# Where the sums of v's weights are made: from the first v product, four parts of 1024 columns, to the first u and g product, eight parts of 512

## The chip, the cores and the metric

The kernel runs on one core of a Trainium2 chip. The metric is the device time of one execution in microseconds (us), as the median of several runs. The engines are named as in the profile: PE is TensorE's matmul side, PEld its weight loads, DVE is VectorE, ACT is ScalarE, POOL is GpSimd, SP is SyncE, which here only issues DMAs. L12 is line 12 of the kernel file. Lines of the changed file are given with the words "of the changed kernel", since they are shifted by one or by six.

## The reference

Two layers act on x of 2048 tokens by 1024 features. The first is a gated MLP whose gate mixes the tokens of a chunk, the second is windowed attention. Only the first matters here:

```python
z = h @ w_in                       # 2048x1024 @ 1024x6144
u, v, g = jnp.split(z, 3, axis=-1) # 2048 wide each
v = layer_norm(v, ln_g, ln_b)
sv = jnp.einsum('gts,bcsgd->bctgd', wsm, v) + bs...   # per chunk of 128 tokens
y = u * sv * jax.nn.silu(g)
return y @ w_out
```

`h` is the RMS norm of x. Everything is float32, with an error that asks for more than one float32r pass.

## The kernel before

**Precision.** Every operand of a large product is split into a high float32r part (a CAST on ACT) and a low part (a subtraction on DVE); `split` does both, L118 and L119. A product is then three matmuls: high by high, high by low, low by high.

**Seven products for eight.** Most products are made as two by two blocks with seven block products (`chain_of`, L519), named "11", "12", "s2", "s1", "s3", "s4", "22". The blocks of both sides have first to be added and subtracted. For x, and for the gated y, this is `combos` (L365): four POOL operations (L373, L375, L379, L381) with seven DMAs that store the results (L367). For the weights of u, g and the output product it is done on POOL as they are fetched (L223 to L226, four operations for each weight tile).

**The order of the first layer.** The tokens are taken in two halves, `sb` 0 and 1.

- The first v product (`vphase_first`, L591) has no combinations: 64 steps of 12 matmuls each, one weight tile of 128x512 a step. Meanwhile x is loaded and normed, and `x_steps` (L424) makes x's combinations for the later products (DVE L451 and L452, then `combos`).
- The first u and g product follows: eight calls of `ug_pair` (L642), called a pair below, each with 14 weight tiles of 12 matmuls. In a pair, the previous pair's gate is worked out (`mix`, L628, with PE L635 and DVE L637, L639, L640) and its y combined on POOL (`combos`). In each of the fourth to seventh pair one quarter of the second half's x is combined as well (`x_steps(1, k)`, DVE L448, POOL `combos`).
- The output product, and then the same for `sb` = 1, whose v product (`vphase`, L573) is made with seven block products. Its weights' sums are read from `sumD` in DRAM. They are what the change moves.

**The sums of v's weights.** `sum_job(i)` (L465), i from 0 to 3, loads four blocks of w_v of 128x1024 into two large tiles `qa` (the places of x's "11" set, which is not loaded yet), and after two steps `quarter_sums` (L475) does four operations with two POOL instructions each (L479) and stores each result with one DMA issued by POOL (L472). That is 32 POOL operations and 16 POOL DMAs in all. They are kept in an order of their own by `in_turn`.

**What sets the order.** `after(n, fn)` calls `fn` n steps later; a step is one call of `half()`, that is 12 matmuls. Tile code emits instructions in that order, and a scheduler then fixes the row of each engine. Each engine takes its row strictly in order. Weight tiles are fetched three steps ahead (`LOOKAHEAD`), with four buffers `wa` of split weights (`W_BUFS`) and twelve of raw ones (`RAW_A`). Small tiles of 128x512 called `s` come from a pool of 18 (`GEN_A`); a load into such a tile waits on SP's row until the tile's former user is through, and what stands behind it on SP waits too.

```python
        for i in range(4):
            after(14 + 9 * i, lambda i=i: sum_job(i))          # L785, within the first v product
        ...
        for k in range(4):
            for i, f in enumerate(x_steps(1, k, None)):
                after(14 * (k + 3) + 5 + i, f)                 # L811, within the first u and g product
```

Of the kernel before, what the change touches and what calls it, by code (L numbers as in the profile page):

```python
# [12 lines left out]
F32 = mybir.dt.float32  # L13
# [3 lines left out]
ALU = mybir.AluOpType  # L17

P = 128
# [32 lines left out]
PLAIN = ("11", "12", "21", "22")  # L52
PIECES = "k00 k01 q00 q01 g00 q10 q11 g01 q20 q21 g10 q30 q31 g11 g20 g21 g30 g31".split()
ATT = [11, 12, 14, 15, 18, 20, 20, 22, 23, 26, 28, 28, 29, 31, 33, 35]
S_T = 4
T_PV = 3
K_T = 5
# [5 lines left out]
def trunk(ctx: ExitStack, tc: tile.TileContext, xT, wv, wug, wao, wkv, wqg, wbo, wsT, bs, gains, lngb,  # L63
          bq, bkv, sinks, rot, masks, out):
    nc = tc.nc
    V, A, G, PE = nc.vector, nc.scalar, nc.gpsimd, nc.tensor

    glob = ctx.enter_context(tc.tile_pool(name="glob", bufs=1))
    xcg = ctx.enter_context(tc.tile_pool(name="xcg", bufs=1))
# [10 lines left out]
    sumD = [[dram.tile([P, 2, 512], F32, name=f"su{i}_{n}", tag=f"su{i}_{n}") for n in range(4)] for i in range(4)]  # L80
# [7 lines left out]
    def load(dst, src):  # L88
        nc.sync.dma_start(dst, src)

    def slot(dt=F32):
        return gen[0].tile([P, TB], dt, name="s", tag="s")
# [49 lines left out]
    def after(n, fn):  # L142
        at(now[0] + n, fn)
# [18 lines left out]
    for b in range(NB):  # L162
        for p in PIECES:
            kind, i, j = p[0], int(p[1]), int(p[2])
# [168 lines left out]
    with ExitStack() as actx:  # L333
# [128 lines left out]

            return [begin, lambda: None, lambda: None, lambda: norms(0), lambda: norms(1), step, step, step]

        def sum_job(i):  # L465

            t = [xcg.tile([P, 2048], F32, name="qa", tag=tag) for tag in ("11h", "11l")]
            a11, a12, a21, a22 = (t[z // 2][:, (z % 2) * 1024:(z % 2 + 1) * 1024] for z in range(4))
            for t, q in ((a21, 2), (a22, 3), (a11, 0), (a12, 1)):
                load(t.rearrange("p (u c) -> p u c", u=2),  # L470
                     wv[i // 2, q, 2 * (i % 2):2 * (i % 2) + 2].rearrange("u p c -> p u c"))
            after(2, lambda: quarter_sums(a11, a12, a21, a22, lambda n, t: G.dma_start(  # L472
                sumD[i][n], t.rearrange("p (u c) -> p u c", u=2))))

        def quarter_sums(a11, a12, a21, a22, put):  # L475
            def tt(out, a, b, op):
                for z in range(2):
                    zs = slice(z * 512, (z + 1) * 512)
                    in_turn(lambda: G.tensor_tensor(out[:, zs], a[:, zs], b[:, zs], op))  # L479

            tt(a22, a21, a22, ALU.add)
            put(0, a22)
            tt(a21, a11, a21, ALU.subtract)
            put(2, a21)
            tt(a11, a22, a11, ALU.subtract)
            put(1, a11)
            tt(a12, a12, a11, ALU.subtract)
            put(3, a12)


        pre_jobs = [(wkv[i], wkvD[i], kv_g[:, 4 * i:4 * i + 4], 4) for i in range(2)]
# [265 lines left out]
        def in_turn(fn):  # L757

            if gl[0] is None:
                gl[0] = fn().ins  # L760
                return
            with tc.issue_after(gl[0]):
                gl[0] = fn().ins
# [17 lines left out]
        for k in range(KD):  # L781
            after(1 + k // 2, lambda k=k: ys.append(first_x(1, k)))
            after(3 + k // 2, lambda k=k: first_split(1, k, ys[k]))
            after(6 + k // 2, lambda k=k: first_stat(1, k, ys[k], 2))
        for i in range(4):  # L785
            after(14 + 9 * i, lambda i=i: sum_job(i))
        for k in range(4):
            for i, f in enumerate(x_steps(0, k, ("12h", "12l", "s2h", "s2l")[k])):
                after(17 + 8 * k + i, f)
# [6 lines left out]
        for sb in range(2):  # L796
# [8 lines left out]
            pend = None  # L805
            res = {}
            if sb == 0:
                for b in range(2, 4):
                    for i, f in enumerate(stat_steps(b)):
                        after(3 + 16 * (b - 2) + 3 * i // 2, f)  # L810
                for k in range(4):  # L811
                    for i, f in enumerate(x_steps(1, k, None)):
                        after(14 * (k + 3) + 5 + i, f)
# [321 lines left out]
    for b in range(NB):  # L1135
# [15 lines left out]
        def attend(i, b=b, qT=qT, os_=os_, finish_quad=finish_quad):  # L1151
# [14 lines left out]

            after(S_T, second)

        for i in range(16):
            at(h0 + ATT[i], lambda i=i, f=attend: f(i))  # L1170
        if b + 1 < NB:
# [3 lines left out]
        for p in PIECES:  # L1175
            kind, i, j = p[0], int(p[1]), int(p[2])
# [79 lines left out]
```

## Time and profile before

| what | value |
|---|---|
| median of 3 runs | 2219.04 us (2216.8 to 2220.34) |
| the profiled execution | 2223.57 us, its span 2221.8 us, 1.8 us lie around it |
| granted TensorE clock, mean | 0.983 |
| first v product | from 5.6 to 226.1 us of the span |
| first u and g product | from 226.1 to about 563 us |
| POOL operations L479 | 32, from 30.0 to 147.4 us, median 1404 ns |
| POOL DMAs L472 | 16, median 579 ns to issue, median 4.0 us to land |

In a row of the timeline stand the start and the length in us, then engine, line, operation, the tile that is written and the tile that is read, and the count of merged instructions; in brackets the idle time of the engine ahead of it and what ended it. A row of windows has the length of the stretch, for each engine its busy time with the number of instructions, the granted clock of TensorE, the busy share of the 16 DMA engines and GB/s. A row of groups ends with the busy time and the mean length in ns of one instruction, and then the idle time ahead of it.

### The profile page before, as it was taken

What the parts mean: (1) busy time and instruction counts of PE and PEld (TensorE: products, weight loads), DVE (VectorE), ACT (ScalarE), POOL (GpSimd) and SP (SyncE); (2) the same over time, 40 slices, a digit from 0 to 9 for tenths busy, and PEclk for the clock granted to TensorE, in tenths of its full rate; (3) what the DMA queues carried; (4) which work ended last, traced back from release to release, by engine and by line L of the source; (5) the groups of instructions that cost most, each with busy time, mean ns of one, the idle gap of its engine ahead of it and who ended that gap; (6) DMA issues with size and microseconds to landing.
All of it is one profiled execution on the core that took longest, in us unless ns stands there. A gap on an engine that the chain in (4) does not pass through costs nothing.

```text
span 2221.8 us, 33592 instructions
## 1 busy us (share of the span) xinstructions
PE 2133.6 (96%) x11196; PEld 1809.7 (81%) x11196; DVE 1687.7 (76%) x2693; ACT 1089.2 (49%) x2431; POOL 1065.4 (48%) x1178
## 2 busy tenths in 40 slices
PE   7799999999899999999999899999999999999997
PEld 5578888888688777788888688898899889889986
DVE  9976778888986865766657987578867967986785
ACT  5225654445444534545444543257535834663573
POOL 3781446767544566644544445334415613451460
PEclk8899999999999999999999999999999999999999
DMA  8997555667786799634435796542463354346322
GB/s 290 318 348 243 169 183 182 197 209 242 265 297 224 265 326 330 211 117 147 154 110 157 250 324 206 197 141 102 140 225 114 127 195 163 114 128 243 115 96 95
DMA packets 208940, 441.95 MB, mean 199 GB/s; under 512 B 22656, under 2 KB 61824, under 8 KB 199552
## 3 DMA queue, kind: packets, MB, share of 16 engines
q1 hardware_dynamic: 163488, 255.76, 35.6%
q0 software_dynamic: 40672, 175.66, 21.7%
q10 hardware_dynamic: 4608, 8.39, 1.0%
q8 instruction: 89, 1.46, 0.3%
q14 instruction: 83, 0.68, 0.1%
HBM read 322.81 MB, written 116.92 MB: 198 GB/s over the span
## 4 chain that ended last, share of the span: by engine, by line
PE 45%; DVE 8%; issue 3%; ACT 2%; DMA 2%; POOL 1%; SPq 0%; DVEq 0%; POOLq 0%; ACTq 0%
PE ps L122 7%; PE ps L124 6%; PE ps L123 6%; PE ps L130 6%; PE ps L129 6%; PE ps L128 6%; PE ps L1019 2%; PE ps L997 1%; PE ps L635 1%; PE ps L966 1%; PE ps L967 1%; PE ps L938 1%; DVE hn L119 1%; DVE o L1027 1%; DVE wa L119 1%
## 5 line engine op out<-in xcount | busy, mean ns | idle before, releaser
L119 DVE TENSOR_TENSOR wa<-w_raw,wa 128x512 fp32r<-128x512 f32 x456 | 465.2, 1029 | 156.4 <-ACT wa L118 153.2
L130 PE MATMUL ps<-xh,wa 128*128 128x512 f32 x1344 | 529.5, 394 | 17.7 <-DVE wa L119 17.7
L128 PE MATMUL ps<-xh,wa 128*128 128x512 f32 x1344 | 530.9, 395 | 1.3 <-ACT s L549 1.0
L129 PE MATMUL ps<-xl,wa 128*128 128x512 f32 x1344 | 527.9, 393 | 0.0
L118 ACT CAST wa<-w_raw 128x512 fp32r<-128x512 f32 x456 | 280.5, 618 | 405.8 <-PE ps L130 303.7
L130 PEld LDWEIGHTS ps<-xh,wa 128*128 128x128 f32 x1344 | 253.2, 188 | 78.7 <-DVE wa L119 22.4
L128 PEld LDWEIGHTS ps<-xh,wa 128*128 128x128 f32 x1344 | 253.5, 189 | 57.1 <-ACT s L549 1.4
L129 PEld LDWEIGHTS ps<-xl,wa 128*128 128x128 f32 x1344 | 253.4, 189 | 55.6
L1005 POOL TENSOR_SCALAR_AFFINE_SELECT s<-s 128x512 fp32r<-128x512 f32 x256 | 185.3, 752 | 101.8 <-ACT s L999 69.5
L122 PE MATMUL ps<-w,hn 128*128 128x256 f32 x640 | 184.2, 288 | 0.0
L223 POOL TENSOR_TENSOR w_raw<-w_raw 128x512 f32<-128x512 f32 x48 | 75.0, 1565 | 226.0 <-DMA w_raw<-in_wug 134.3
L123 PE MATMUL ps<-w,hn 128*128 128x256 f32 x640 | 182.3, 285 | 0.0
L124 PE MATMUL ps<-w,hn 128*128 128x256 f32 x640 | 182.2, 285 | 0.0
L119 DVE TENSOR_TENSOR xl<-s,xh 128x512 fp32r<-128x512 f32 x168 | 137.4, 853 | 15.0 <-ACT xh L118 14.5
L190 POOL DMA_DIRECT2D w<-wb x72 | 40.6, 565 | 208.3 <-PE ps L124 182.6
L631 ACT ACTIVATE vp<-vp,nb,rs 128x128 f32<-128x128 f32 x256 | 106.7, 485 | 56.6 <-DMA vp<-v 47.8
L991 POOL TENSOR_TENSOR s<-s,rd 128x512 f32<-128x512 f32 x64 | 69.6, 1090 | 115.1 <-ACT s L999 47.0
L123 PEld LDWEIGHTS ps<-w,hn 128*128 128x128 f32 x640 | 124.0, 194 | 0.5
L122 PEld LDWEIGHTS ps<-w,hn 128*128 128x128 f32 x640 | 124.0, 194 | 0.5
L124 PEld LDWEIGHTS ps<-w,hn 128*128 128x128 f32 x640 | 123.9, 194 | 0.0
L123 PE MATMUL ps<-wa,xh 128*128 128x512 f32 x256 | 104.7, 409 | 19.0 <-DVE wa L119 18.9
L225 POOL TENSOR_TENSOR w_raw<-w_raw 128x512 f32<-128x512 f32 x48 | 66.3, 1386 | 103.2 <-DVE wa L119 102.2
(190 smaller groups left out, 5011.4 us busy)
## 6 DMA issues: line engine op xcount, KB each, us to landing
w<-wb POOLq DMA_DIRECT2D x72, 1024.0 KB, 5.3
w_raw<-in_wug SPq DMA_DIRECT2D x160, 256.0 KB, 3.3
w_raw<-in_wv SPq DMA_DIRECT2D x88, 256.0 KB, 5.4
s<-in_xT SPq DMA_DIRECT2D x80, 256.0 KB, 4.8
w_raw<-in_wao SPq DMA_DIRECT2D x80, 256.0 KB, 4.1
wb<-s POOLq DMA_DIRECT2D x72, 256.0 KB, 5.8
vp<-v SPq DMA_DIRECT2D x32, 512.0 KB, 4.6
Y_s<-s POOLq DMA_DIRECT2D x64, 256.0 KB, 3.9
```

The source lines that it names most:

```text
L118: A.copy(hi, src)
L119: (lo_eng or V).tensor_tensor(lo, src, hi.bitcast(F32), ALU.subtract)
L122: PE.matmul(ps, ah, bh, start=first, stop=False)
L123: PE.matmul(ps, ah, bl, start=False, stop=False)
L124: PE.matmul(ps, al, bh, start=False, stop=last)
L128: PE.matmul(ps, ah, bh, start=first, stop=False, skip_group_check=True)
L129: PE.matmul(ps, ah, bl, start=False, stop=False, skip_group_check=True)
L130: PE.matmul(ps, al, bh, start=False, stop=True, skip_group_check=True)
L223: G.tensor_tensor(u["22"], u["21"], u["22"], ALU.add)
L631: A.activation(v[:, c, :], v[:, c, :], AF.Identity, bias=nb[:, c:c + 1], scale=rs[:, c:c + 1])
L991: G.tensor_tensor(p4, p4, rd[:, :, None].broadcast_to([P, 4, P]), ALU.mult)
L1005: G.affine_select(out=y.rearrange("p (h q) -> p h q", h=4), in_=x.rearrange("p (h q) -> p h q", h=4), pattern=[[0, 4], [sign, P]], base=ba ...
```

## The change

The four jobs of 1024 columns become eight of 512, `sum_job(i, u)`. They use four tiles `s` each in place of the two large ones. Their steps are listed in `SUMS`, counted from the start of the first u and g product: 37 and 41 lie at the end of the third pair, 55 and 58 around the border of the fourth and fifth, 69 and 72 of the fifth and sixth, 83 and 86 of the sixth and seventh. The sums follow three steps after the loads. The 32 POOL operations stay 32, each of the same size; the POOL DMAs become 32, of 256 KB in place of 512 KB; the loads become 32 of 256 KB in place of 16 of 512 KB. `in_turn` is no longer used for them.

```diff
+SUMS = (37, 41, 55, 58, 69, 72, 83, 86)
...
-        def sum_job(i):
-            t = [xcg.tile([P, 2048], F32, name="qa", tag=tag) for tag in ("11h", "11l")]
-            a11, a12, a21, a22 = (t[z // 2][:, (z % 2) * 1024:(z % 2 + 1) * 1024] for z in range(4))
+        def sum_job(i, u):
+            a11, a12, a21, a22 = (slot() for _ in range(4))
             for t, q in ((a21, 2), (a22, 3), (a11, 0), (a12, 1)):
-                load(t.rearrange("p (u c) -> p u c", u=2),
-                     wv[i // 2, q, 2 * (i % 2):2 * (i % 2) + 2].rearrange("u p c -> p u c"))
-            after(2, lambda: quarter_sums(a11, a12, a21, a22, lambda n, t: G.dma_start(
-                sumD[i][n], t.rearrange("p (u c) -> p u c", u=2))))
...
+                load(t, wv[i // 2, q, 2 * (i % 2) + u])
+            def tt(n, out, a, b, op):
+                G.tensor_tensor(out, a, b, op)
+                G.dma_start(sumD[i][n][:, u, :], out)
+            def sums():
+                tt(0, a22, a21, a22, ALU.add)
+                tt(2, a21, a11, a21, ALU.subtract)
+                tt(1, a11, a22, a11, ALU.subtract)
+                tt(3, a12, a12, a11, ALU.subtract)
+            after(3, sums)
...
-        for i in range(4):
-            after(14 + 9 * i, lambda i=i: sum_job(i))
...
             if sb == 0:
+                for i in range(8):
+                    after(SUMS[i], lambda i=i: sum_job(i // 2, i % 2))
```

POOL's row early in the first v product, before. `r_474` and `r_650` are the inverse norms of the two token blocks, `su` a stored sum, `X` a stored combination of x:

```order
L119 TENSOR_TENSOR s<-s 128x512
L260 TENSOR_TENSOR r_474<-m_471,neghalf 128x4
L479 TENSOR_TENSOR qa<-qa 128x512 x2
L472 DMA su_0_153<-qa 128x1024
L479 TENSOR_TENSOR qa<-qa 128x512 x3
L472 DMA su_2_155<-qa 128x1024
L479 TENSOR_TENSOR qa<-qa 128x512 x2
L472 DMA su_1_154<-qa 128x1024
L479 TENSOR_TENSOR qa<-qa 128x512
L472 DMA su_3_156<-qa 128x1024
L119 TENSOR_TENSOR s<-s 128x512
L367 DMA X_11_169<-xq 128x512
```

Here a whole job of eight operations and four stores stands between the two norms, and more of them follow behind each other down to the end of the row's part for the v product. The same place in the changed kernel:

```order
L120 TENSOR_TENSOR s<-s 128x512
L261 TENSOR_TENSOR r_474<-m_471,neghalf 128x4
L120 TENSOR_TENSOR s<-s 128x512
L368 DMA X_11_169<-xq 128x512
L261 TENSOR_TENSOR r_650<-m_647,neghalf 128x4
L368 DMA X_12_170<-xq 128x512
```

Nothing is left between the two norms but the split of the second one's sum.

POOL's row where the fifth pair begins, before. `X_22` is the last store of x's combinations of the pair before, `w_raw` the weights of u and g (L225 makes what "s2" multiplies, L226 what "s4" does, L223 and L224 belong to the next pair):

```order
L380 TENSOR_TENSOR s<-s 128x512
L367 DMA X_s_180<-s 128x512
L381 TENSOR_TENSOR s<-s 128x512
L367 DMA X_22_182<-s 128x512
L225 TENSOR_TENSOR w_raw<-w_raw 128x512 x2
L226 TENSOR_TENSOR w_raw<-w_raw 128x512 x2
L223 TENSOR_TENSOR w_raw<-w_raw 128x512
L224 TENSOR_TENSOR w_raw<-w_raw 128x512
L367 DMA Y_0_11_183<-s 128x512
```

The four operations on the weights follow each other here. The same place in the changed kernel, where L473 and L474 are the sums and their stores, and L226 and L227 the former L225 and L226; the first of the two jobs that stand here is shown:

```order
L368 DMA X_22_182<-s 128x512
L226 TENSOR_TENSOR w_raw<-w_raw 128x512
L473 TENSOR_TENSOR s<-s 128x512
L226 TENSOR_TENSOR w_raw<-w_raw 128x512
L474 DMA su_0_157<-s 128x512
L473 TENSOR_TENSOR s<-s 128x512
L474 DMA su_2_159<-s 128x512
L473 TENSOR_TENSOR s<-s 128x512
L227 TENSOR_TENSOR w_raw<-w_raw 128x512
L474 DMA su_1_158<-s 128x512
L473 TENSOR_TENSOR s<-s 128x512
L474 DMA su_3_160<-s 128x512
```

Eight sums and eight stores now stand between the first L225 of a pair and the L223 of the next; the same is found at the starts of the sixth and seventh pair, and at the start of the fourth the two jobs begin just ahead of the first L225.

SP's row at the same place in the changed kernel; before, the rows are the same without the one that reads `in_wv`, and all five `w_raw` follow each other:

```order
L90 DMA w_raw<-in_wug 128x512 x4
L90 DMA s<-in_wv 128x512 x8
L90 DMA w_raw<-in_wug 128x512
L90 DMA vp<-v_2_143 128x8x128
L90 DMA w_raw<-in_wug 128x512
```

The eight loads of two jobs stand in a row, ahead of a raw weight tile. The tiles that they fill were last read by stores of y's and x's combinations, and the next x loads in turn fill tiles that the sums' stores read.

More of the change, by code (lines that the diff above doesn't have):

```diff
@@ L463, in x_steps @@
             return [begin, lambda: None, lambda: None, lambda: norms(0), lambda: norms(1), step, step, step]
-        def sum_job(i):
-            t = [xcg.tile([P, 2048], F32, name="qa", tag=tag) for tag in ("11h", "11l")]
-            a11, a12, a21, a22 = (t[z // 2][:, (z % 2) * 1024:(z % 2 + 1) * 1024] for z in range(4))
+        def sum_job(i, u):
+            a11, a12, a21, a22 = (slot() for _ in range(4))
             for t, q in ((a21, 2), (a22, 3), (a11, 0), (a12, 1)):
-                load(t.rearrange("p (u c) -> p u c", u=2),
-                     wv[i // 2, q, 2 * (i % 2):2 * (i % 2) + 2].rearrange("u p c -> p u c"))
-            after(2, lambda: quarter_sums(a11, a12, a21, a22, lambda n, t: G.dma_start(
-                sumD[i][n], t.rearrange("p (u c) -> p u c", u=2))))
[L475 to L488, printed above, removed]
+                load(t, wv[i // 2, q, 2 * (i % 2) + u])
[8 more added lines that the diff above has]
+            after(3, sums)
         pre_jobs = [(wkv[i], wkvD[i], kv_g[:, 4 * i:4 * i + 4], 4) for i in range(2)]
```

## The prediction, on record before the run

> **What bounds the kernel now.** I read the page first, then the windows of the two places that the change touches, then their timelines.
>
> ```profile
> span 2221.8 us, 33592 instructions
> PE 2133.6 (96%) x11196; PEld 1809.7 (81%) x11196; DVE 1687.7 (76%) x2693; ACT 1089.2 (49%) x2431; POOL 1065.4 (48%) x1178
> ```
>
> PE bounds the whole: a change pays only where it takes idle time, or a low clock, from PE. The windows show where that is. First four stretches of the first v product, from which the sums go, then the fourth to seventh pair, to which they come:
>
> ```profile
> 25.00:50.00 25.00, 17.11 (x63) 13.38 (x64) 24.08 (x26) 10.95 (x19) 14.83 (x13) 0.80 0.87 310
> 50.00:75.00 25.00, 15.36 (x55) 11.24 (x54) 21.09 (x25) 4.21 (x7) 17.48 (x15) 0.85 0.66 218
> 75.00:100.00 25.00, 25.00 (x102) 19.73 (x100) 25.00 (x32) 8.21 (x13) 15.98 (x17) 0.94 0.94 329
> 100.00:125.00 25.00, 16.58 (x62) 12.49 (x61) 23.11 (x22) 4.91 (x8) 20.91 (x24) 0.86 0.94 328
> 349.60:394.30 44.70, 44.70 (x212) 37.18 (x211) 37.20 (x37) 21.19 (x43) 29.80 (x32) 1.00 0.62 209
> 394.30:440.20 45.90, 45.90 (x218) 38.17 (x217) 37.65 (x40) 21.02 (x43) 30.37 (x31) 1.00 0.62 204
> 440.20:482.10 41.90, 41.90 (x200) 34.78 (x199) 33.52 (x35) 19.20 (x41) 28.86 (x30) 1.00 0.67 219
> 482.10:523.60 41.50, 41.50 (x199) 34.55 (x198) 35.96 (x37) 19.67 (x40) 29.43 (x30) 1.00 0.68 223
> ```
>
> In the v product PE idles and its granted clock falls to 0.80, while DVE is busy 21 to 25 of 25 us. In the pairs PE is never idle; DVE is busy 80 to 87%, POOL 66 to 71%. PE's timeline has these gaps up to 226 us:
>
> ```profile
> 42.13 0.80 PE L123 MATMUL ps<-wa,xh 128*128 128x512 f32 x1 [7.89 <-DVE wa L119]
> 54.01 0.80 PE L123 MATMUL ps<-wa,xh 128*128 128x512 f32 x1 [2.63 <-DVE wa L119]
> 73.73 0.80 PE L288 MATMUL ps<-s,ones_r 128*128 128x512 f32 x1 [6.71 <-DVE s L282]
> 101.84 0.51 PE L123 MATMUL ps<-wa,xh 128*128 128x512 f32 x1 [1.43 <-DVE wa L119]
> 111.87 0.79 PE L123 MATMUL ps<-wa,xh 128*128 128x512 f32 x1 [6.99 <-DVE wa L119]
> ...
> 46.99 0.43 PE L123 MATMUL ps<-wa,xh 128*128 128x512 f32 x1
> ...
> 226.06 0.39 PE L128 MATMUL ps<-xh,wa 128*128 128x512 f32 x1
> 226.29 0.39 PE L129 MATMUL ps<-xl,wa 128*128 128x512 f32 x1
> ```
>
> The gaps add up to 25.7 us, and all end on DVE. After a long gap the clock is low: the eleven matmuls that start from 42.13 up to 46.99 take 4.9 us, where at full clock they start 0.23 us apart (226.06 to 226.29) and would take 2.6. So each long gap costs 2.3 us more. Four such make 9.2 us, and the whole loss is 34.9 us. Why DVE is late stands in its timeline and in POOL's groups:
>
> ```profile
> 33.05 5.01 DVE L279 TENSOR_TENSOR r4l<-r,r4h 128x4 f32<-128x4 f32 x1
> 41.40 0.68 DVE L119 TENSOR_TENSOR wa<-w_raw,wa 128x512 fp32r<-128x512 f32 x1
> 43.68 0.68 DVE L119 TENSOR_TENSOR wa<-w_raw,wa 128x512 fp32r<-128x512 f32 x1
> 53.27 2.48 DVE L119 TENSOR_TENSOR wa<-w_raw,wa 128x512 fp32r<-128x512 f32 x4
> 64.03 7.32 DVE L277 CAST r4h<-r 128x4 fp32r<-128x4 f32 x1 [2.18 <-POOL r L260]
> 101.71 8.44 DVE L452 TENSOR_TENSOR xq<-xq,s 128x512 f32<-128x512 f32 x1
> ...
> 33.67 3.71 POOL L479 TENSOR_TENSOR qa<-qa 128x512 f32<-128x512 f32 x3
> ...
> L479 POOL TENSOR_TENSOR qa<-qa 128x512 f32<-128x512 f32 x32 | 45.4, 1461 | 6.7 <-DMA qa<-in_wv 6.5
> L472 POOL DMA_DIRECT2D su<-qa x16 | 9.7, 603 | 0.6 <-POOL qa L479 0.6
> ```
>
> An operation on four columns takes 5.01 and 7.32 us, a sum that takes 0.68 when POOL rests takes 8.44, each while POOL works through sums of v's weights (33.67). Operations of DVE on two SBUF tiles are shut out while POOL computes. I call them locked operations below.
>
> **Part one: 32 sums, 16 POOL DMAs and 16 loads of 512 KB leave the v product.** Gap by gap:
>
> - 42.13: L279 and what follows lose their stretching, and the weight of 41.40 is ready some 8.5 us sooner, when PE asks for it. The gap goes: 7.9 and 2.3.
> - 54.01: this one does not go. Between the weights of 43.68 and of 53.27 DVE's row holds 16 other operations, with POOL at rest. The third weight comes 53.27 - 41.40 = 11.9 us after the first. PE uses up two in 2 x 12 x 0.23 = 5.6 us; PE may now ask for the first about 1 us after it is ready, so it runs dry for some 5 us in place of 2.6. It costs 2.4 us more.
> - 73.73: the second norm waits for L277's 7.32 us. L277, L279 and L282 then take their usual part of a us; PE, which came at 67.0, finds the data there. 6.7 and 2.3 go. In PE's row the second half of the mean (the former L271) moves up by five matmuls, closer to its POOL split: up to 2 us against that.
> - 101.84 and 111.87: the second is L452's 8.44 us and goes (7.0 and 2.3). The first lies among x's combinations, which stay on POOL; I let it stand.
>
> Gone: 10.2 + 9.0 + 9.3 = 28.5. New: 2.4 + 2. That gives 24; DVE's list becomes denser as PE runs ahead, for which I take off 2. **Gain 22 us**, with bounds 12 (only two of the three long gaps go, and one comes back by a third) and 30.
>
> **Part two: they come to the pairs.** The groups of 330 to 500 us, four pairs:
>
> ```profile
> L119 DVE TENSOR_TENSOR wa<-w_raw,wa 128x512 fp32r<-128x512 f32 x56 | 76.4, 1372 | 19.4 <-ACT wa L118 19.4
> L656 DVE TENSOR_TENSOR s<-ps,s 128x512 f32<-128x512 f32 x24 | 16.2, 678 | 0.0
> L639 DVE TENSOR_TENSOR s<-s 128x512 f32<-128x512 f32 x16 | 15.0, 955 | 0.0
> L640 DVE TENSOR_TENSOR s<-s 128x512 f32<-128x512 f32 x16 | 14.6, 932 | 0.0
> L637 DVE SCALAR_TENSOR_TENSOR s<-ps,lngb_sb,wc 128x512 f32<-128x512 f32 x16 | 11.5, 742 | 2.8 <-PE ps L635 2.8
> L375 POOL TENSOR_TENSOR s<-s 128x512 f32<-128x512 f32 x7 | 9.2, 1313 | 0.1
> ...
> 388.49 3.09 DVE L119 TENSOR_TENSOR wa<-w_raw,wa 128x512 fp32r<-128x512 f32 x1
> ...
> PE ps L128 <- DVE s L656: 0.4, 1, 0.4
> ...
> 400.24 1.95 PE L635 MATMUL ps<-wc,vp 128*128 128x128 f32 x16
> 442.41 1.95 PE L635 MATMUL ps<-wc,vp 128*128 128x128 f32 x16
> ...
> 441.54 0.62 ACT L118 CAST wa<-w_raw 128x512 fp32r<-128x512 f32 x1 [1.06 <-POOL w_raw L225]
> ```
>
> A pair takes 42.2 us (400.24 to 442.41), and PE waited once in four pairs, for 0.4 us. Lock and cover are already there: L119 takes 1372 ns on average and 3.09 us inside x's combinations, while L656, which reads PSUM, keeps its 678.
>
> POOL's bill for two jobs a pair: 8 sums at 1.31 (L375) to 1.46 (L479) = 10.5 to 11.7 us, and 8 DMAs at 0.60 = 4.8: about 16. In the last three of the four stretches POOL is busy 30.4, 28.9 and 29.4 us; with 16 more 45 to 46, in 42.2. It overruns by 3.5 a pair, 10.5 in three. The fourth pair has 44.7 - 29.8 = 14.9 us of idle POOL time for its 16, and adds 1.1. Behind the sums on POOL's row stand L225's second tile, L226, the next pair's L223 and L224, the stores of y and x, and both sets of combinations; PE waits in the end for the weights of "s2". They have slack: the cast of 441.54 is followed by L119's 0.7 to 3.1 us, so they are ready by 445 at worst; the sixth pair begins 442.41 - 5.5 = 436.9, and "11" and "12" of 24 matmuls and two mixes make 14.5 us, so PE asks at 451.4. That is 6 us of cover. So 11.6 - 6 = 5.6 us reach PE, in some three gaps at 2.3 of low clock each: 12. A stall also gives POOL and DVE time, so it does not grow by itself.
>
> The loads, with a row of the stores' landing:
>
> ```profile
> DMA to landing us min/median/max: 2.9/4.0/10.7
> ```
>
> Eight of 256 KB stand on SP ahead of a raw weight. Their tiles come free with stores of the combinations; the next x loads wait for stores of the sums. Each is some 4 us from issue to landing (the row is that of L472), and I see cover for it while POOL is full. In the eighth pair and after nothing is added. **Cost 12 us**, with bounds 0 (the 14.9, 15.5, 13.0 and 12.1 us of idle time are all used, and DVE packs between) and 35 (the loss that these same sums make where they are now).
>
> [...] The row for the stores, by line:
>
> ```profile
> L472 POOL DMA_DIRECT2D su<-qa x16: 539/579/767, 32.9 to 149.7; - x16
> ```
>
> Issue never took over 0.77 us, with DVE busy nearly all of that time. [...]
>
> **The rivals.** All times are medians: the profiled execution's 2223.6 stands 4.5 over the median, and the sums are differences, so I take them from 2219.
>
> - Forecast, 0.38: 22 gained, 12 lost, 2209 us.
> - The pairs take the sums for nothing, 0.22: 22 to 25 gained, 0 to 4 lost, 2196. For it: POOL's idle time of 12 to 15 us a pair, and DVE filling whole stretches before without a stall of PE. Against it: POOL's sum of over 42.2.
> - The gain stays small, 0.18: DVE's own list makes new gaps as PE comes earlier, so 12 are gained and 12 lost, 2219. For it: the gap of 54.01, that POOL has no part in.
> - The lock takes PE's time in the pairs, 0.22, slower. With POOL never idle every locked operation of DVE waits for a whole POOL operation. A pair has 14 L119 and 8 of L639 and L640: 22 x (0.68 + 1.31) = 43.8, and 6 L656 and 4 L637 add 7: 50.6 us of DVE in 42.2, 8.4 over. Three pairs make 25, less 6 of cover, and 7 for the clock and 5 in the fourth pair: 31 lost, 22 gained, 2228. It decides from a cost of 26 us on, at some 7 us a pair. Against it: the mean L119 waits 0.7 now, half of that.
>
> [...]
>
> **How the numbers follow.** About 4.4 us (0.2%) can be told from no change. The forecast's own spread is 2203 to 2215; with the second and third case whole, and the fourth to just over its point, the range is 2195 to 2229. Faster: the first two cases, 0.60. Same: 0.18. Slower: 0.22.
>
> **What would show it.** In the profile after: no wait of over 3 us of PE on DVE in the v product but the one of 54.01, at about 40 to 45 us; the first L128 near 204 in place of 226.06. In the pairs POOL busy over 95% of the time from the fifth pair on, L119 at 1.7 to 2 us on average, waits of PE on L119 of 5 to 10 us in all, mostly in the sixth and seventh. If L128 comes at 204 and the pairs keep 42.2, the second case holds; if they take 48 and more, the last. If L128 comes after 213, part one is wrong.

## The result and the profile after

The changed kernel takes 2235.3 us (median of 4 runs, 2230.9 to 2237.0), the kernel before 2219.7 (4 runs, 2216.8 to 2220.5). The ratio is 1.007, with a 95% interval from 1.0052 to 1.0088: slower by some 15.6 us, on the other side of the forecast and 6 us beyond its range. The profiled execution took 2236.4 us, its span is 2234.7.

Lines below are those of the changed kernel: L120 is the low part of a split on DVE (L119 before), L131 a matmul of the u and g product (L130), L633 and L634 the gate's two products (L639, L640), L473 a sum and L474 its store, L224 to L227 the sums of the u and g weights on POOL.

**The v product.** PE's row on the timeline, from 40 us on, and where the u and g product begins. In brackets is the wait and what ended it.

```profile
44.26 0.50 PE L124 MATMUL ps<-wa,xh 128*128 128x512 f32 x1 [2.65 <-DVE wa L120]
47.18 0.79 PE L272 MATMUL ps<-s,inv_r 128*128 128x512 f32 x1 [1.73 <-POOL s L120]
...
199.96 0.39 PE L129 MATMUL ps<-xh,wa 128*128 128x512 f32 x1
```

Of the five gaps shown before, only that of 54.01 is left, now 2.65 us long; a wait of 1.73 us at the norm's matmul is new. The u and g product begins at 199.96 us in place of 226.06: 26.1 us gained.

**The pairs.** Windows of the third to seventh pair, from the start of one mix to the next. The columns are length, busy time of PE, PEld, DVE, ACT and POOL with instruction counts, the granted clock, the DMA share and GB/s.

```profile
287.80:331.50 43.70, 43.51 (x206) 35.89 (x205) 31.68 (x40) 20.67 (x42) 23.18 (x23) 1.00 0.56 187
331.50:381.90 50.40, 45.61 (x202) 37.06 (x201) 42.12 (x35) 19.28 (x40) 41.11 (x45) 0.93 0.74 246
381.90:435.40 53.50, 46.47 (x201) 36.96 (x200) 44.48 (x38) 19.35 (x40) 41.56 (x46) 0.94 0.74 250
435.40:491.50 56.10, 45.75 (x201) 35.70 (x200) 49.57 (x36) 19.16 (x40) 44.49 (x49) 0.94 0.72 240
491.50:544.50 53.00, 45.40 (x201) 35.80 (x200) 47.97 (x37) 20.59 (x42) 43.76 (x47) 0.97 0.69 232
```

The third pair is as before. The four pairs with sums take 50 to 56 us in place of 42.2. POOL is busy 78 to 83% of that, not 95%; DVE is busy 42 to 50 us. So POOL does not overrun. The waits of PE on DVE in the whole run, and those of ACT on POOL for the sums that "s2" multiplies (total, times, longest):

```profile
PE ps L131 <- DVE wa L120: 45.2, 29, 7.1
...
ACT wa L119 <- POOL w_raw L226: 1.2, 2, 0.8
```

The chain that the forecast priced ran from POOL's row over L226 to ACT's cast and so to PE. ACT waited there for 1.2 us in all.

The groups from 330 to 540 us answer to those of 330 to 500 before (L119 1372 ns, L639 955, L640 932, L656 678):

```profile
L120 DVE TENSOR_TENSOR wa<-w_raw,wa 128x512 fp32r<-128x512 f32 x54 | 107.5, 2003 | 16.5 <-ACT wa L119 16.5
L633 DVE TENSOR_TENSOR s<-s 128x512 f32<-128x512 f32 x16 | 22.8, 1446 | 0.0
L634 DVE TENSOR_TENSOR s<-s 128x512 f32<-128x512 f32 x16 | 19.7, 1250 | 0.0
L650 DVE TENSOR_TENSOR s<-ps,s 128x512 f32<-128x512 f32 x24 | 16.3, 678 | 0.0
```

The low parts of the weights and the gate's two products, which have two inputs in SBUF, have become longer, by 630, 490 and 320 ns; L650, which reads PSUM, has not. How it comes about, on DVE's and on POOL's row:

```profile
377.21 1.83 DVE L120 TENSOR_TENSOR wa<-w_raw,wa 128x512 fp32r<-128x512 f32 x1
378.98 6.52 DVE L120 TENSOR_TENSOR wa<-w_raw,wa 128x512 fp32r<-128x512 f32 x1
385.42 5.29 DVE L120 TENSOR_TENSOR wa<-w_raw,wa 128x512 fp32r<-128x512 f32 x1
390.64 0.68 DVE L120 TENSOR_TENSOR wa<-w_raw,wa 128x512 fp32r<-128x512 f32 x1
```

```profile
379.37 1.30 POOL L226 TENSOR_TENSOR w_raw<-w_raw 128x512 f32<-128x512 f32 x1
380.62 1.29 POOL L473 TENSOR_TENSOR s<-s 128x512 f32<-128x512 f32 x1
381.86 1.27 POOL L226 TENSOR_TENSOR w_raw<-w_raw 128x512 f32<-128x512 f32 x1
383.07 0.56 POOL L474 DMA_DIRECT2D su<-s  x1
383.65 1.28 POOL L473 TENSOR_TENSOR s<-s 128x512 f32<-128x512 f32 x1
385.24 0.56 POOL L474 DMA_DIRECT2D su<-s  x1 [0.30 <-POOL s L473]
385.82 1.31 POOL L473 TENSOR_TENSOR s<-s 128x512 f32<-128x512 f32 x1
387.07 1.30 POOL L227 TENSOR_TENSOR w_raw<-w_raw 128x512 f32<-128x512 f32 x1
388.30 0.56 POOL L474 DMA_DIRECT2D su<-s  x1
388.88 1.27 POOL L473 TENSOR_TENSOR s<-s 128x512 f32<-128x512 f32 x1
390.45 0.56 POOL L474 DMA_DIRECT2D su<-s  x1 [0.30 <-POOL s L473]
```

Four subtractions that take 0.68 us each when POOL rests take 14.1 together. In the rows shown POOL does seven additions, one right behind the other or with a pause for a store: about 0.5 us where the store need not wait, 0.9 us where it waits 0.30. The second and third subtraction end in the two pauses of 0.9 us (at 385.50 and 390.71) and let those of 0.5 us go by. The second lasts through four additions of POOL. PE uses up a weight tile in 2.8 us (12 matmuls 0.23 us apart), and DVE makes one in 3.5.

**The balance.** From the first matmul of the u and g product to out_pair's first mix (591.33 us; 572.30 before). First before, then after:

```profile
226.06:572.30 346.24, 342.13 (x1602) 282.93 (x1601) 285.50 (x326) 185.76 (x374) 202.20 (x192) 1.00 0.63 204
```

```profile
199.96:591.33 391.37, 357.01 (x1601) 288.05 (x1600) 325.15 (x329) 184.08 (x373) 258.82 (x255) 0.97 0.67 223
```

The stretch has grown by 45.1 us: 14.9 of them are PE's own longer busy time at the lower clock, 30.2 are waits. On DVE's side, its busy time has grown by 39.7, and the rest of the stretch from 60.7 to 66.2. With 26.1 gained, 19.0 are lost at that point; the two spans differ by 12.9. The part behind it took 1637.6 to 1649.5 us in the seventeen profiles of this case, all with the same code there, and 1649.5 is the value of before: the 6 us between 19.0 and 12.9 are of the size of that scatter.

### The profile page after: what moved, and what is told of

The parts are those of the page before. It is cut to its first block, busy times and chain, and to the rows that moved or that the text cites. A ratio compares the mean times of both kernels' runs of the same rounds, so it can differ in the third digit from the quotient of the medians.

```text
span 2234.7 us, 33669 instructions
## 1 busy us (share of the span) xinstructions
PE 2142.3 (96%) x11196; PEld 1811.6 (81%) x11196; DVE 1693.0 (76%) x2693; ACT 1087.7 (49%) x2431; POOL 1068.5 (48%) x1194
## 4 chain that ended last, share of the span: by engine, by line
PE 64%; DVE 16%; issue 8%; DMA 5%; ACT 3%; POOL 3%; SPq 1%; DVEq 0%; POOLq 0%; ACTq 0%
PE ps L131 10%; PE ps L130 10%; PE ps L129 10%; PE ps L123 9%; PE ps L124 9%; PE ps L125 8%; DVE wa L120 3%; PE ps L1013 2%; PE ps L629 1%; DVE s L633 1%; PE ps L991 1%; PE ps L960 1%; DVE xl L120 1%; PE ps L961 1%; PE ps L932 1%
## 5 line engine op out<-in xcount | busy, mean ns | idle before, releaser
L120 DVE TENSOR_TENSOR wa<-w_raw,wa 128x512 fp32r<-128x512 f32 x456 | 486.1, 1075 | 163.0 <-ACT wa L119 162.1
L131 PE MATMUL ps<-xh,wa 128*128 128x512 f32 x1344 | 536.3, 399 | 45.2 <-DVE wa L120 45.2
L129 PE MATMUL ps<-xh,wa 128*128 128x512 f32 x1344 | 535.2, 398 | 0.8 <-ACT s L543 0.6
L130 PE MATMUL ps<-xl,wa 128*128 128x512 f32 x1344 | 532.2, 396 | 0.0
L119 ACT CAST wa<-w_raw 128x512 fp32r<-128x512 f32 x456 | 280.2, 618 | 390.3 <-PE ps L131 292.1
L131 PEld LDWEIGHTS ps<-xh,wa 128*128 128x128 f32 x1344 | 255.9, 190 | 115.1 <-DVE wa L120 58.8
L129 PEld LDWEIGHTS ps<-xh,wa 128*128 128x128 f32 x1344 | 256.1, 191 | 56.8 <-ACT s L543 1.0
L130 PEld LDWEIGHTS ps<-xl,wa 128*128 128x128 f32 x1344 | 255.9, 190 | 56.7
L224 POOL TENSOR_TENSOR w_raw<-w_raw 128x512 f32<-128x512 f32 x48 | 73.2, 1527 | 221.3 <-DMA w_raw<-in_wug 140.2
L120 DVE TENSOR_TENSOR xl<-s,xh 128x512 fp32r<-128x512 f32 x168 | 137.6, 857 | 14.5 <-ACT xh L119 14.3
L985 POOL TENSOR_TENSOR s<-s,rd 128x512 f32<-128x512 f32 x64 | 69.6, 1090 | 114.2 <-DVE rd L983 44.9
L226 POOL TENSOR_TENSOR w_raw<-w_raw 128x512 f32<-128x512 f32 x48 | 69.0, 1440 | 98.3 <-DVE wa L120 87.4
L119 ACT CAST xh<-s 128x512 fp32r<-128x512 f32 x168 | 97.3, 617 | 37.4 <-DMA s<-Y 10.3
```

Of the source, the lines that this page charges most:

```text
L119: A.copy(hi, src)
L120: (lo_eng or V).tensor_tensor(lo, src, hi.bitcast(F32), ALU.subtract)
L129: PE.matmul(ps, ah, bh, start=first, stop=False, skip_group_check=True)
L130: PE.matmul(ps, ah, bl, start=False, stop=False, skip_group_check=True)
L131: PE.matmul(ps, al, bh, start=False, stop=True, skip_group_check=True)
L224: G.tensor_tensor(u["22"], u["21"], u["22"], ALU.add)
```

## The experiments

In the table, "stretch" runs from the first matmul of the u and g product to out_pair's first mix, both read off PE's timeline in the one profile of each kernel; DVE is its busy time there, "rest" the stretch less that. Ratios are to the kernel before on the same chip in the same session (its median there 2217 to 2220), with a 95% interval; of the experiments, those without one ran once.

| kernel | sums made by, where | us | ratio | u and g from | stretch | DVE | rest |
|---|---|---|---|---|---|---|---|
| before | POOL, v product | 2219.7 | | 226.1 | 346.2 | 285.5 | 60.7 |
| after | POOL, pairs 3 to 7 | 2235.3 | 1.007 (1.0052 to 1.0088) | 200.0 | 391.4 | 325.2 | 66.2 |
| e1_no_sums | nobody, loads and stores as after | 2193.2 | | 199.2 | 351.8 | 285.9 | 65.9 |
| e2_dve | DVE, as after | 2206.2 | 0.9946 (0.9929 to 0.9963) | 198.5 | 365.4 | 305.0 | 60.4 |
| e3_late_v | POOL, second half of v product | 2210.8 | 0.9966 (0.9953 to 0.9979) | 212.6 | 348.5 | 294.1 | 54.4 |
| e4_half | POOL, as after, every second job | 2222.4 | | 199.0 | 373.7 | 303.8 | 69.9 |
| e5_dve_late_v | DVE, second half of v product | 2208.8 | 0.9949 (0.9930 to 0.9968) | 209.2 | 353.7 | 292.7 | 61.0 |
| e6_one_a_pair | POOL, one job a pair, ahead of the mix | 2244.8 | 1.0107 (1.0086 to 1.0129) | 198.9 | 401.9 | 289.2 | 112.7 |
| e7_memset | two memsets for each sum, as after | 2208.9 | | 198.6 | 362.0 | 281.9 | 80.1 |
| e8_dve_one_a_pair | DVE, places of e6 | 2220.9 | 1.0006 (0.9992 to 1.0020) | 199.5 | 376.6 | 305.6 | 71.0 |
| e9_dve_early | DVE, pairs 1 to 3 | 2209.2 | 0.9957 (0.9942 to 0.9972) | 199.9 | 362.9 | 312.7 | 50.2 |
| e10_pool_early | POOL, pairs 1 to 3 | 2232.9 | 1.0057 (1.0035 to 1.0079) | 199.2 | 385.4 | 327.7 | 57.7 |
| e11_dve_early_store | as e9, later stores | 2207.0 | 0.9947 (0.9930 to 0.9963) | 198.5 | 364.6 | 313.1 | 51.5 |
| e12_memset_long | three memsets for each sum, as after | 2213.2 | | 198.8 | 370.3 | 272.8 | 97.5 |
| e13_pause | POOL, as after, a memset behind each | 2230.9 | 1.0057 (1.0039 to 1.0076) | 198.6 | 390.0 | 318.8 | 71.2 |
| e14_dve_seven | DVE, one job a pair, places as after | 2194.1 | 0.9895 (0.9869 to 0.9921) | 199.1 | 354.4 | 308.9 | 45.5 |
| e15_pool_seven | POOL, places of e14 | 2225.6 | 1.0021 (1.0010 to 1.0033) | 199.1 | 384.1 | 337.5 | 46.6 |

The theory (A below): POOL's additions shut DVE's two-input operations out, and PE waits for the weights that DVE makes. The rivals: the new loads, tiles and stores (B), or that DVE simply has no room for more work (C).

**e1_no_sums.** The additions go, everything else stays.

```diff
-                G.tensor_tensor(out, a, b, op)
```

> The 32 additions on POOL are left out; the raw quarters are stored in their place, so the second v product works with wrong weights. Loads, tiles and the 64 stores by POOL stay where the change put them. Theory A (the additions shut DVE's two-input SBUF operations out, and PE waits for DVE's weights): the seven pairs lose their extra time, from 391.6 us for the stretch from the first u and g matmul to out_pair's first mix to 346 to 354; L120 back to about 1.4 us on average there; 2235.3 - 45.4 + 6 (which the kernel won back later) = 2196, 2192 to 2206. Theory B (the eight loads on SP, the tiles s that they hold, the stores on POOL's queue): the stretch stays at 375 to 392, 2222 to 2236.

The stretch, by windows, and the DVE groups in it:

```profile
199.15:550.96 351.81, 345.43 (x1601) 283.73 (x1600) 285.87 (x324) 183.35 (x373) 219.32 (x224) 1.00 0.74 248
```

```profile
L120 DVE TENSOR_TENSOR wa<-w_raw,wa 128x512 fp32r<-128x512 f32 x112 | 138.3, 1246 | 33.5 <-ACT wa L119 33.4
L633 DVE TENSOR_TENSOR s<-s 128x512 f32<-128x512 f32 x28 | 24.7, 902 | 0.0
L632 DVE TENSOR_TENSOR s<-s 128x512 f32<-128x512 f32 x28 | 24.4, 891 | 0.0
```

351.8 us, as A has it: the additions cost 391.4 - 351.8 = 39.6 us, and loads, tiles and stores at most 5.6 over before. DVE is busy as long as before, and the clock stays at 1.00.

**e2_dve.** The same sums at the same places, on DVE.

```diff
-                G.tensor_tensor(out, a, b, op)
+                V.tensor_tensor(out, a, b, op)
```

> The additions stay at their eight places in the pairs and go from POOL to DVE; the stores stay on POOL. Theory A (the lock): DVE gets 8 x 0.65 to 0.75 us = 5 to 6 us a pair more, which is less than the 42.2 - 38 or so that it had idle or shut out, and nothing of POOL's shuts it out; the stretch of the pairs is 346 to 358 us, 2193 to 2210. Theory B (loads, tiles, stores): the stretch stays at 375 to 392, 2222 to 2236. Theory C (DVE has no room for any work more, whoever does the additions): half of the loss stays, 365 to 375, 2212 to 2224.

```profile
L120 DVE TENSOR_TENSOR wa<-w_raw,wa 128x512 fp32r<-128x512 f32 x112 | 123.0, 1107 | 19.4 <-ACT wa L119 19.4
L473 DVE TENSOR_TENSOR s<-s 128x512 f32<-128x512 f32 x32 | 35.3, 1104 | 8.5 <-DMA s<-in_wv 7.9
```

The time is in A's range, the stretch of 365.4 in C's. 26.0 of the 39.6 us go with the engine alone, though DVE now has 35.3 us more work: here it costs DVE less to do the additions itself (305.0 us busy) than to be shut out by them (325.2). 13.6 stay; e14 takes up most of them.

**e3_late_v and e5_dve_late_v.** The eight jobs move to the second half of the v product, on POOL and on DVE.

```diff
-SUMS = (37, 41, 55, 58, 69, 72, 83, 86)
+SUMS = (36, 39, 42, 45, 48, 51, 54, 57)
...
+        for i in range(8):
+            after(SUMS[i], lambda i=i: sum_job(i // 2, i % 2))   # at the head of the v product
```

> The additions are on POOL again, in eight parts as after the change, but in the second half of the first v product (from 127 us on POOL is idle there for most of 69 us, and DVE is busy 10.5 to 18 of 25 us). Theory A (the lock costs only where DVE has no idle time to make it up): the v product ends 0 to 8 us later than after the change (first L129 at 200 to 208), the pairs take 42.2 us again, 2193 to 2208. If additions on POOL cost PE the same wherever they are (32 x 1.3 us of exclusion), 20 us or more come back: 2210 to 2225.

> As e3 (eight parts in the second half of the first v product), with the additions on DVE instead of POOL. In e3 the first u and g matmul came at 212.6 us, 13 later than after the change. Lock theory: these 13 us are DVE's operations shut out by a nearly unbroken row of POOL's additions (one turn per addition and store, 2.17 us); on DVE the 32 additions take 32 x 0.65 = 21 us of about 28 that it has idle there: first u and g matmul at 199 to 205, pairs 346 to 350 us, 2193 to 2203. Rival: the DMAs make PE wait (their share is 0.96 to 1.02 from 100 to 213 us in e3, 350 to 374 GB/s): first u and g matmul at 209 to 214, 2206 to 2213.

The same two windows near the v product's end, e3 first, then e5; the last two columns are the DMA share and GB/s:

```profile
150.00:175.00 25.00, 20.48 (x86) 15.55 (x84) 25.00 (x14) 8.57 (x15) 23.94 (x28) 1.00 1.02 374
175.00:200.00 25.00, 18.51 (x65) 14.55 (x66) 22.23 (x21) 8.29 (x14) 20.34 (x21) 0.86 0.96 339
```

```profile
150.00:175.00 25.00, 21.66 (x93) 16.92 (x92) 16.33 (x20) 7.20 (x12) 8.92 (x13) 1.00 0.95 350
175.00:200.00 25.00, 21.62 (x91) 16.52 (x89) 17.59 (x30) 9.90 (x17) 9.71 (x13) 1.00 1.03 386
```

In the pairs little of the loss is left in both (348.5 and 353.7 us). But the u and g product begins 9 to 13 us later than after the change, on either engine, and my expectation for both was wrong. In e3 DVE is busy without a break in the first window, with 14 instructions in 25 us, so the exclusion is at work there too. In e5 it is busy only 16 to 18 of 25 us, and PE still stands still 3.3 and 3.4 us, with a DMA share of 0.95 and 1.03. From 100 to 213 us of e5 DVE waits 11.1 us for the loads of the sums, and ACT 19.1 us for loads of x's combinations. So the rival of e5 fits: its loads come late. That the DMAs' share is the reason is argued from these numbers, not tested, and in e3 the two causes are not separated.

**e4_half.** Only the second job of each pair adds.

```diff
-                G.tensor_tensor(out, a, b, op)
+                if u:
+                    G.tensor_tensor(out, a, b, op)
```

> Every second job leaves its additions out and stores raw quarters, so that each pair has four additions in place of eight; half of the second v product works with wrong weights. Theory A with DVE as a list that overflows: 4 x 1.3 us of exclusion a pair mostly fits into DVE's idle time, the loss is far less than half, 0 to 12 of the 45 us: 2193 to 2206. A loss in proportion to the additions: 22 us, 2211 to 2217. Theory B: 2222 to 2236.

The stretch is 373.7: 21.9 us for 16 additions, 1.37 each, against 39.6 / 32 = 1.24 for all. The loss is in proportion from the first addition on, not small until DVE's idle time is used up. That part of A was wrong. The one run of 2222 us lies above the proportional range; with e1 at 2193, B is not an explanation for it, and the stretch speaks for proportion.

**e6_one_a_pair and e8_dve_one_a_pair.** One job to a pair, ahead of the mix.

```diff
-SUMS = (37, 41, 55, 58, 69, 72, 83, 86)
+SUMS = (4, 9, 23, 37, 51, 65, 79, 93)
```

> POOL's additions again, all of them, but one job to a pair in seven pairs (two in the first), and ahead of the mix rather than in it. e4 lost 21.7 us to 16 additions in four pairs, 1.36 each, 5.4 a job. Theory A0 (in the last pairs DVE is full, and each addition costs its 1.3 us wherever it stands): four jobs there at 5.4 and up to 5 each for the other four: the stretch of the pairs is 374 to 392, 2216 to 2234. Theory A1 (the loss arises where a dense row of POOL meets the mix's eight two-input operations of DVE and the weights; spread out, DVE makes it up in idle time of 6 to 10 us a pair): 355 to 366, 2198 to 2209.

> As e6, with the additions on DVE. e2 (two jobs a pair in four pairs, on DVE) took 365.5 us for the pairs, 13.7 over e1 without additions. A1: 352 to 358, 2195 to 2203. A0 in its form for DVE (0.43 us lost to each addition of 1.1): 360 to 366, 2201 to 2209.

e6 is the slowest of all, yet its DVE time is only 3.3 us over that of e1. The groups of its stretch, with the idle time ahead of them in the last column:

```profile
L120 DVE TENSOR_TENSOR wa<-w_raw,wa 128x512 fp32r<-128x512 f32 x113 | 138.1, 1230 | 79.5 <-ACT wa L119 79.5
L473 POOL TENSOR_TENSOR s<-s 128x512 f32<-128x512 f32 x32 | 41.6, 1301 | 28.4 <-DMA s<-in_wv 27.9
```

This is a second mechanism, the one on which the forecast's 12 us rested (POOL's row delays the weights' sums). POOL takes its row in order and stands still 28 us for the loads of the sums, and the weights' sums stand behind. Then ACT waits for them, in the whole run by this row, where it was 1.2 us after the change:

```profile
ACT wa L119 <- POOL w_raw L226: 29.1, 7, 6.6
```

And DVE waits for ACT (79.5 us in place of 33.5). In e8 it is DVE that waits 27 us for these loads. Both kernels came out beyond all the ranges of their expectations, so they don't answer the question that they were made for (does spreading help); e14 and e15 come closer. After the change POOL waits for these loads 6 us, so that this is not what the change lost by.

**e7_memset and e12_memset_long.** POOL's time without POOL's reading.

```diff
-                G.tensor_tensor(out, a, b, op)
+                for _ in range(2):          # e12: range(3)
+                    G.memset(out, 0.01)
```

> Each of POOL's 32 additions is replaced by two memsets of the same tile: POOL's queue is held, but nothing is read from SBUF; the second v product works with wrong weights. If an addition costs by the time that it takes on POOL's queue (the sums of the u and g weights stand behind it), the stretch of the pairs stays over 375 us, provided that two memsets take about as long as an addition's 1.3 us, and in proportion if less. If it costs by the exclusion of DVE, and that needs a POOL operation that reads SBUF: 350 to 357, L120 near 1.25 us on average, 2192 to 2202. If writing alone excludes too: L120 and L633 are stretched as after the change, 375 to 392.

> As e7, at the change's own places, with three memsets for each addition: 32 x 1.62 = 52 us of POOL, more than the 42.5 that the additions take, but nothing is read from SBUF; the second v product works with wrong weights. e7 lost 9.8 us (361.6 for the pairs) with 32 to 34 us of memsets. If POOL's time is what costs, the loss is at least that of the additions: pairs over 388, 2232 and more. If the exclusion of DVE costs: 358 to 374, 2206 to 2218, with L633 and L634 at 0.9 to 1.05 us on average.

e7, POOL's row and DVE's row at the same time, in the first mix with memsets (L634, L635 are the gate's products there):

```profile
335.95 1.92 POOL L474 MEMSET s<- 128x512 f32 x4
337.83 1.09 POOL L475 DMA_DIRECT2D su<-s  x2
338.92 1.94 POOL L474 MEMSET s<- 128x512 f32 x4
```

```profile
337.14 0.68 DVE L120 TENSOR_TENSOR wa<-w_raw,wa 128x512 fp32r<-128x512 f32 x1
337.74 0.68 DVE L634 TENSOR_TENSOR s<-s 128x512 f32<-128x512 f32 x1
...
339.01 0.68 DVE L635 TENSOR_TENSOR s<-s 128x512 f32<-128x512 f32 x1
339.61 0.68 DVE L634 TENSOR_TENSOR s<-s 128x512 f32<-128x512 f32 x1
```

And e12, its stretch and the memsets in it:

```profile
198.79:569.10 370.31, 350.12 (x1602) 285.46 (x1600) 272.80 (x328) 184.03 (x373) 262.34 (x320) 0.99 0.72 238
```

```profile
L474 POOL MEMSET s<- 128x512 f32 x96 | 47.4, 539 | 6.9 <-DMA s<-in_wv 6.8
```

Under the memsets of these rows DVE's two-input operations take 0.68 us. The stretch of e7, 362.0, lies between the two ranges of its expectation; that of e12 lies in the range for the exclusion. 31.9 us of memsets cost 362.0 - 351.8 = 10.2 us, 47.4 cost 18.5, all in DVE's rest (80 and 98 us) and none in its busy time: this is put down to the queue, POOL's own time, at 0.3 to 0.4 of it. DVE's waits for ACT are 44.9 and 44.8 us in place of 33.5; the rest of what e12 lost was not followed further. The additions, with 42.5 us, less than e12's memsets, cost 39.6, and all of it as DVE's busy time. So the exclusion is the larger part. In these runs POOL's additions, which read SBUF, shut DVE out (L120 took up to 6.52 us), and its memsets, which only write, did not (0.68); a POOL operation with a single input was not tried.

**e9_dve_early, e10_pool_early, e11_dve_early_store.** The jobs in the first three pairs, where the change had lost nothing.

```diff
-SUMS = (37, 41, 55, 58, 69, 72, 83, 86)
+SUMS = (1, 4, 7, 10, 13, 16, 27, 30)
...
-                G.dma_start(sumD[i][n][:, u, :], out)                    # e11
+                after(2, lambda: G.dma_start(sumD[i][n][:, u, :], out))  # e11
```

> The additions on DVE, and in the first three pairs in place of the last four: four jobs in the first pair, two in the second and two in the third, where nothing was lost after the change (44.3, 43.8, 43.7 us; DVE is busy 31 to 36 us in each, POOL 17 to 23, the DMAs 0.5 to 0.6 of the time). Theory (an addition costs what DVE's idle time and the DMAs in its pair don't cover): 32 x 0.65 to 0.8 = 21 to 26 us of DVE in some 30 us of idle time: pairs 348 to 358 us, 2196 to 2206. Rival (DVE and POOL each take their work in order, and stand still for the loads and for one another's results: 27 and 48 us of such waits in e8): 362 to 375, 2208 to 2220.

> The additions on POOL, at the same early places as e9. Theory: 42 us of exclusion against some 30 us of DVE's idle time and 20 us of POOL's in each pair: pairs 356 to 370, 2203 to 2218, well under the change's own 391.6. Rival (each addition costs its 1.3 us wherever it stands): 385 to 395, 2228 to 2240.

> As e9, with each store issued by POOL two steps after its addition, so that POOL, which takes its work in order, does not stand still at the store with the sums of the u and g weights behind it. If that wait costs: 3 to 10 us less than e9. If not: the same within 3 us.

e10, DVE's row in the first pair:

```profile
217.57 16.45 DVE L120 TENSOR_TENSOR wa<-w_raw,wa 128x512 fp32r<-128x512 f32 x4
```

On POOL the additions cost 33.6 us over e1 here too, 1.05 each, in pairs in which DVE had 8 to 13 us of idle time: the rival of e10 holds, and my view of idle time as a reserve is wrong for POOL's additions in a row. Four of DVE's operations took 16.45 us together; the third of them, while POOL did four additions:

```profile
222.14 6.51 DVE L120 TENSOR_TENSOR wa<-w_raw,wa 128x512 fp32r<-128x512 f32 x1
```

On DVE (e9) it is 11.1 us over e1, at the lower end of the rival's ranges: POOL stood 28 us at stores of sums that DVE had not made yet. e11 says nothing: POOL waited for DVE's sums 28.2 us in it, 28.4 in e9, so the edit did not take the wait away.

**e13_pause.** A memset right behind each addition.

```diff
+                with tc.issue_after(done.ins):      # done: the addition
+                    G.memset(rest, 0.0)
```

> The kernel after the change, with a memset of 448 columns of a tile of its own right behind each of the 32 additions (0.47 us each by e7's 0.54 for 512: 15 us more work for POOL). In e7 memsets did not shut DVE out, so each is a pause in which DVE may have a turn, beside the store's 0.56 us. Theory T (DVE gets its turn only in POOL's pauses, so it suffers from how rarely POOL pauses): L120, L633 and L634 get shorter on average than after the change (1447, 1236 and 1094 ns), the pairs take 370 to 389 us in place of 391.6, 2213 to 2233. Theory M (DVE is shut out for as long as POOL reads, in sum, and the order of the two matters little): L120 stays at 1400 to 1500, the pairs take 392 to 402, 2235 to 2246.

15.4 us more work for POOL, and the stretch is 390.0, 1.4 shorter than after the change: between the two ranges, with the time of 2230.9 in T's. L120 takes 1399 ns in its stretch, the gate's second product 1008, the first 1236. That leans to T and does not decide. The memset came next to the store, so it made the pauses longer that were there, and a sum of the u and g weights could still stand between it and the addition. 52 times in this stretch an addition of POOL follows another within 0.1 us, as often as after the change.

The rows of the kernel after, from 199.96 to 591.33 us, say more. The cases are counted in which a TENSOR_TENSOR of DVE with all its inputs in SBUF was still held up when an addition of POOL ended. It was through by the start of the next addition, to within 0.05 us, in all 61 cases with a pause of 0.6 us or more, in 4 of 12 with a pause of about 0.5 us, and in none of 41 where the next addition came within 0.1 us. In e10 it is 68 of 68, 0 of 6 and 0 of 43. So a turn for DVE depends on a pause of POOL that is long enough; this is a count on two traces, not an experiment.

**e14_dve_seven and e15_pool_seven.** Two jobs in the first pair, one in each pair after, at the places in a pair that the change uses; DVE, and POOL.

```diff
-SUMS = (37, 41, 55, 58, 69, 72, 83, 86)
+SUMS = (1, 5, 13, 27, 41, 55, 69, 83)
```

> The additions on DVE, one job to a pair from the second pair on and two in the first, at the places in a pair where the change has them (in e8 they stood just ahead of the mix, and DVE waited 27 us for their loads). If the loss of e2 (13.7 us over e1 for two jobs a pair in four pairs) comes from two jobs close together: pairs 353 to 360, 2195 to 2203. If each addition on DVE costs its 0.4 us wherever it is: 363 to 368, 2204 to 2210.

> As e14 (pairs in 354.6 us, 2194), with the additions on POOL: only the engine differs. If an addition on POOL costs 1.25 us wherever it stands among the pairs, as in e1 against after, e4 and e10: pairs 386 to 394, 2226 to 2238. If one job to a pair at these places fits into DVE's idle time, so that the change's fault was two jobs close together: 355 to 368, 2195 to 2210.

The stretch by windows and L120 in it, of e14:

```profile
199.09:553.50 354.41, 345.40 (x1601) 283.64 (x1600) 308.89 (x355) 185.36 (x374) 219.75 (x224) 1.00 0.73 246
```

```profile
L120 DVE TENSOR_TENSOR wa<-w_raw,wa 128x512 fp32r<-128x512 f32 x112 | 134.4, 1210 | 14.6 <-ACT wa L119 14.6
```

And of e15:

```profile
199.14:583.26 384.12, 352.68 (x1602) 284.22 (x1601) 337.51 (x325) 185.00 (x373) 260.75 (x257) 0.99 0.68 227
```

```profile
L120 DVE TENSOR_TENSOR wa<-w_raw,wa 128x512 fp32r<-128x512 f32 x112 | 171.7, 1545 | 22.3 <-ACT wa L119 19.2 <-DMA s<-in_wv 3.0
```

The stretch of the four combinations, beside the 351.8 of e1:

| | POOL | DVE | by the engine |
|---|---|---|---|
| two jobs a pair, four pairs | 391.4 | 365.4 | 26.0 |
| one job a pair, seven pairs | 384.1 | 354.4 | 29.7 |
| by the place | 7.3 | 11.0 | |

e14 came out as the crowding theory has it, e15 just below the range for 1.25 us an addition. The engine is worth 26 to 30 us and the places 7 to 11. Whether it is the crowding of two jobs that costs these 7 to 11 is not separated: e14 and e15 also move half of the jobs out of the four pairs that lost time after the change. DVE's idle time can be used, some 20 us of it in both spread kernels (rest 46 in place of 66); but POOL's additions add 52 us to DVE's busy time there, DVE's own 23. e14 is faster than both kernels: 2194.1 us, 1% under before, with this line of `SUMS` and the one line of e2 as its edits. In its profile out_pair's first mix comes 18.8 us earlier than before; the rest of its gain lies behind that point, where the scatter is of this size.

## Why the prediction was wrong

- **Part one, the gain of 22 us: right,** 26.1 measured, within the bounds of 12 to 30. The gaps of 42.13, 73.73 and 111.87 went, and that of 101.84, which was let stand, went too. The gap of 54.01 came at 44.26 as said, but did not grow to 5 us (2.65; the row of DVE between the two weights has 15 operations, not 16). The norm's matmul waited 1.73 of "up to 2", and the 2 us taken off for a denser list of DVE were not needed.
- **Part two, the cost of 12 us in the pairs: this step failed;** 45.1 measured, beyond the upper bound of 35. The pairs were priced by POOL's overrun of its own row, and the exclusion of DVE, though seen, was put at nothing. Four things in it:
  - "It overruns by 3.5 a pair": POOL did not. It was busy 78 to 83%, and ACT waited only 1.2 us for the sums of L226, the path by which the overrun was to reach PE. The bill was made for POOL's time; e7 and e12 show that POOL's time alone costs 0.3 to 0.4 of itself.
  - The lock was seen ("Lock and cover are already there") and not put into the sum. I took it for a thing that idle time pays. e4, e10 and e15 show 1.0 to 1.4 us of stretch lost to each addition, at three different sets of places among the pairs.
  - "6 us of cover" and "a stall also gives POOL and DVE time": the rest of DVE's time did not shrink (60.7 before, 66.2 after). In part DVE's idle time is a wait for ACT's next cast (30.4 us of it in the stretch after), which does not make up for a turn missed before.
  - Low clock: three gaps at 2.3 us were counted, 7 in all. PE's busy time grew by 14.9, at clocks of 0.93 to 0.97 in four pairs full of short waits.
- **The loads:** "I see cover for it" was about right, 5.6 us at most (e1). It depends on the place: e6 and e8 lose far more by it.
- **The fourth rival, "the lock takes PE's time in the pairs": the mechanism is right, its size was not.** It gave 31 us lost and 2228 (its 43.8 and 7 make 50.8, not 50.6). For the fifth to seventh pair it had 25, less 6 of cover, and 7 for the clock, 26 in all; over the 42.2 of before they lost 36.0. For the fourth pair it had 5; that lost 8.2. The clock took twice its 7, and the cover of 6 does not show. That the pairs took 50.4 to 56.1 us, close to its 50.6, is in part luck: the operations that it adds up kept DVE busy for some 44 us a pair, and L120's mean of 2.0 us is made of operations of 0.68 and of up to 6.52. The rival was given 0.22 on the ground that the mean L119 waited 0.7 us, "half of that". That mean was taken with POOL at 66 to 71%: where additions of POOL follow each other directly, the wait is no longer one POOL operation but several. That every operation waits for one whole POOL operation, 1.31 us, was an estimate that no run shows: L120 took from 0.68 us, with no wait, up to 6.52 us after the change and 6.51 in e10, each through four of POOL's additions.
- **"Operations of DVE on two SBUF tiles":** L277, whose 7.32 us the prediction cites, is a CAST of one tile. It lasted through four of POOL's sums, which points to an exclusion that is not confined to two inputs; no run tests that. And they were not shut out whatever POOL computed: under e7's memsets they took 0.68 us.
- **POOL's time to issue a DMA,** put into its bill at 0.60 us: L474 took 542 to 562 ns, with DVE busy over 80% of these pairs.

## What to carry to other kernels

Where POOL and DVE both work on SBUF operands and DVE feeds the engine that bounds the stage, add the time of POOL's new additions to DVE's busy time before you move work to an "idle" POOL: 42 us of additions made it 39 to 52 us longer than in e1 (after, e10, e15). It was not so where DVE had another wait to pass: in e6, where it stood waiting for ACT's casts for 79.5 us, it was 3.3 us. The same additions on DVE (0.8 to 1.1 us in place of 1.3) can be cheaper even when DVE is the busier engine. Put such jobs where their loads have landed, since both engines take their rows in order: POOL stood still 28 us for them in e6, DVE 27 in e8 (e15 against e6: a stretch of 384.1 and 401.9 us).

## What the runs showed of the hardware

- A waiting TENSOR_TENSOR of DVE got in at every pause of 0.6 us or more between two additions of POOL (61 cases after the change, 68 in e10), at 4 of 18 pauses of about 0.5 us, and never where the additions followed each other within 0.1 us (41 and 43 cases). How much of the loss longer pauses would win back is left open by e13.
- A memset on POOL (0.54 us for 128x512) did not hold DVE up: beside e7's memsets L120, L634 and L635 took 0.68 us.
- Where PE waited often the granted clock fell: 0.93 to 0.97 in the four pairs (45.2 us of waits on DVE in the run), 1.00 over the stretch of e1 (20.4 us). The sum of the waits does not settle it: PE stood still for 31.4 us of e15's stretch at a clock of 0.99, and for 28.7 us of e10's at 0.96.
- The part of the run that no kernel here touched takes 1637.6 to 1649.5 us from profile to profile; two single runs tell nothing below 0.5%.
